# Weight-pair sums in nine steps with their rests on VectorE, and the input's sums made beside the second mLSTM head

## The chip, the cores and the metric

The kernel runs on one core of a Trainium2 chip. A core has five engines with an instruction queue each: TensorE (PE; its weight loads are shown as PEld), VectorE (DVE), ScalarE (ACT), GpSimd (POOL) and SyncE (SP), which here issues most of the DMAs. The metric is the device time of one execution in microseconds, as a median over runs.

## What is computed

One inference step of a hybrid decoder layer: an RMS norm, one input projection `w_in`, then two groups of heads side by side (four mLSTM heads, four HGRN2 heads), an output projection and a SwiGLU feed-forward layer. It is done for a prompt (1 x 1024 tokens) and for samples (8 x 4 tokens) that carry a state.

```python
h = _rmsnorm(x, norm_mix)
p = jnp.einsum('btd,dp->btp', h, w_in) + b_in
qk_a, v_a, o_a, i_a, f_a, q_b, f_b, i_b, g_b = jnp.split(p, offs, axis=-1)
out_a, buf, C, n, m = _mlstm_mixer(qk_a, v_a, o_a, i_a, f_a, conv_buf, C0, n0, m0, conv_w, conv_b, mlstm_norm)
out_b, S = _hgrn_mixer(q_b, f_b, i_b, g_b, S0, lb, hgrn_norm)
mix = jnp.concatenate([out_a, out_b], axis=-1).astype(x.dtype)
x = x + jnp.einsum('btm,md->btd', mix, w_out)
h2 = _rmsnorm(x, norm_ffn)
ff = jax.nn.silu(jnp.einsum('btd,df->btf', h2, w_gate)) * jnp.einsum('btd,df->btf', h2, w_up)
x = x + jnp.einsum('btf,fd->btd', ff, w_down)
```

The change lies in the input projection `w_in` and in what prepares its operands.

## The kernel before

All matrix products are done in fp32 precision by three passes of a rounded format: each operand is cut into a rounded part (`HI`, `whi`) and its rest (`LO`, `wlo` = operand minus rounded part), and PE does HI x whi (L168), LO x whi (L169), HI x wlo (L170). ACT makes the rounded part, and DVE or POOL subtracts to make the rest.

The weights come as tiles of 128 x 1024. `load` issues the DMA of a tile to one of two `raw` buffers (L105, on SP); `split` rounds it in two halves (L96 on ACT) and takes the rests (L97, on POOL or DVE). A tile's load can only go out when all readers of an earlier tile in its raw buffer are through. `nexts` says which tile is loaded after which.

PE's work is a list of units, one per weight tile and token block (1056 tokens in blocks of 288, 384 and 384). `emit_k` issues a unit's matmuls, and after every second step of k calls `hook`, which advances the side work: Python generators (heads, splits, sums) that issue instructions to the other engines and then say with `yield n` after how many hooks they want to go on. So the place of a `yield` sets where in each engine's queue an instruction stands. All engines work their queues in order.

The units go through the four mLSTM heads first (up to about 305 us), then the HGRN heads (up to about 600 us), then the output projection and the feed-forward layer. For the HGRN heads a pair of weight tiles and two token blocks are multiplied by a Strassen scheme of seven products. It needs sums of the inputs and sums of the weights:

- `x1_prep` makes the input's sums T1, T2 and T4 in four turns: it stores part of the input to DRAM (`d_b`), loads blocks of it into tiles that the heads use too (`qB`, `kB`; L1082), adds them (L1085, L1091 on DVE), rounds (L1089 on ACT) and takes the rest (L1092, on POOL). `x3_prep` makes T3 in the same way (L1107 to L1111). `x1_prep` is started 18 units before the first HGRN unit, which is beside the third and fourth mLSTM head.
- `pairs_split` makes the weights' sums S1 to S4 in place in the two raw buffers (L137, L141, L142, L146 on DVE), rounds them (L134 on ACT) and takes their rests (L135 on POOL), in four steps. At its end it loads the next two tiles (called x0 and x1 below). There are six such pairs, starting at about 305, 349, 385, 420, 455 and 490 us.

Of the products, P2's results go to two outputs (`put` L1139 or L1141 on ACT, then `add` L1145 on DVE), P5's are put by ACT (L1139 or L1141), and P3 then goes on in the PSUM bank of P5. Between these products stand the steps of the HGRN heads: decays and products on DVE (L854, L856, L862, L864), small matmuls on PE (L835, L913, L918, L937, L953, L975).

`sample_core` finishes a head for the samples (transpose at L740). `sample_a` does the mLSTM samples: small loads on SP (L754 to L757), then DVE steps (L763, L767, L768) that PE needs (L617). L586 is a memset of one column of `vt` on POOL, L604 a copy of the state C on DVE, L763 the first sample step.

Of the kernel before, what the change touches and what calls it, by code (L numbers as in the profile page):

```python
# [9 lines left out]
F32 = mybir.dt.float32  # L10
# [3 lines left out]
OP = mybir.AluOpType  # L14
# [26 lines left out]
def hybrid_step(ctx: ExitStack, tc: tile.TileContext, i, o):  # L41
    nc = tc.nc
# [9 lines left out]
    def bank(tag="mx"):  # L52
        return psum.tile([128, 512], F32, tag=tag, name=tag, bufs={"mm": 3, "mx": 4, "so": 1}[tag])

    units, tiles, nexts = [], [], {}
# [4 lines left out]
    def start(gen, key, wait=1):  # L60
        active.append([gen, key, wait])
# [12 lines left out]
    def finish(key):  # L74
        while key not in done:
            hook()

    NW, NRAW = 5, 2
    raws, his, los = {}, {}, {}

    def load(t):
        tag = {2: "wlo", 3: "whi"}.get(t, "raw")
        raws[t] = wp.tile([128, 1024], F32, tag=tag, name=tag, bufs=NRAW if tag == "raw" else NW)
        tiles[t](raws[t])
# [18 lines left out]
    def wtile(src, n=1024):  # L103
        def f(raw):
            nc.sync.dma_start(raw[:, :n], src)  # L105
        tiles.append(f)
        tile_n[len(tiles) - 1] = n
        return len(tiles) - 1
# [14 lines left out]
    def pairs_split(tb, ta, raw_a, raw_b):  # L123

        while ("w", raw_b) not in done:
            yield 1
        ra, rb = raws[raw_a], raws[raw_b]
        a11, a12, a21, a22 = ra[:, 0:512], ra[:, 512:1024], rb[:, 0:512], rb[:, 512:1024]

        def rnd(t, s, src):  # L130
            if t not in his:
                his[t] = wp.tile([128, 1024], F32R, tag="whi", name="whi", bufs=NW)
                los[t] = wp.tile([128, 1024], F32R, tag="wlo", name="wlo", bufs=NW)
            nc.scalar.activation(his[t][:, s], src, AF.Copy)  # L134
            nc.gpsimd.tensor_tensor(los[t][:, s], src, his[t][:, s].bitcast(F32), op=OP.subtract)  # L135
        left, right = slice(0, 512), slice(512, 1024)
        nc.vector.tensor_tensor(a22, a21, a22, op=OP.add)  # L137
        yield 1
        rnd(tb, right, a22)
        done.add(("S1", tb))  # L140
        nc.vector.tensor_tensor(a21, a11, a21, op=OP.subtract)  # L141
        nc.vector.tensor_tensor(a11, a22, a11, op=OP.subtract)  # L142
        yield 1
        rnd(ta, left, a11)
        done.add(("S2", tb))
        nc.vector.tensor_tensor(a12, a12, a11, op=OP.subtract)  # L146
        yield 1
        rnd(ta, right, a12)
        done.add(("S4", tb))
        yield 1  # L150
        rnd(tb, left, a21)
        done.add(("S3", tb))
        for x in nexts.get(ta, ()):
            load(x)

    def emit_k(u, ks):
        t, nk = u["t"], u["nk"]
# [123 lines left out]
    def tl(tag, n=384, bufs=2, dt=F32, p=128):  # L281
        n, bufs = 385 if tag == "kB" else n, 3 if tag == "go" else bufs
        return mp.tile([p, n], dt, tag=tag, name=tag, bufs=bufs)
# [253 lines left out]
    def norm_cols(s, sqs, nch, d2=None, p=128):  # L537

        if d2 is None:
            nc.vector.tensor_scalar(s[:p, :nch], sqs[:p, :nch], 1.0 / 128, EPS, op0=OP.mult, op1=OP.add)  # L540
        else:
            nc.vector.tensor_scalar_mul(d2[:p, :nch], d2[:p, :nch], EPS)
            nc.vector.scalar_tensor_tensor(s[:p, :nch], sqs[:p, :nch], 1.0 / 128, d2[:p, :nch],
                                           op0=OP.mult, op1=OP.add)
        nc.gpsimd.tensor_tensor(s[:p, :nch], s[:p, :nch], mhalf[:p, :nch], op=OP.pow)
# [100 lines left out]
    def sample_core(h_off, w, vnorm, st_in, decay, out_state, n_io, d2, k_scale, later=None):  # L646
# [86 lines left out]
            nc.scalar.activation(sm[:, 1, 0:1], pO[:, 128:129], AF.Square)  # L733
            nc.vector.tensor_tensor(sm[:, 1, 0:1], sm[:, 1, 0:1], d2, op=OP.max)
        norm_cols(sm[:, 2], sm[:, 0], 1, sm[:, 1] if d2 is not None else None)
        yield 2
        nc.vector.tensor_scalar_mul(hn, pO[:, 0:128], sm[:, 2, 0:1])
        yield 1
        pH = bank()
        nc.tensor.transpose(pH[:, 0:128], hn, ident)  # L740
        yield 1
# [254 lines left out]
    def sample_b():  # L996
        yield from sample_core(4, 128, V_HN, i["S0"], lambda h, s: gS[:, h, s:s + 1], o["Ss"], None, None, None,
                               later=("su",))
# [15 lines left out]
    for h in range(H):  # L1014
        ts = [wtile(wa[1 + 4 * h + j]) for j in range(4)]
# [15 lines left out]
    first_b = len(units)  # L1031
# [20 lines left out]
    def xop(name):  # L1052
        def blk(b, h_):
            o_ = KT * OFF[b] + 1536 * h_
            return lambda kk: (HI[:, o_ + 384 * kk:o_ + 384 * kk + 384], LO[:, o_ + 384 * kk:o_ + 384 * kk + 384])

        def tx(j):
            return lambda kk: tuple(TX[0][:, 1536 * (2 * j + x) + 384 * kk:1536 * (2 * j + x) + 384 * kk + 384] for x in (0, 1))

        def t4(kk):  # L1060
            return TX[0][:, 6144 + 384 * kk:6528 + 384 * kk], \
                TX[0][:, 7680 + 384 * kk:8064 + 384 * kk] if kk < 2 else t4x[0][:, 384 * kk - 768:384 * kk - 384]
        return {"B11": blk(1, 0), "B21": blk(1, 1), "T3": blk(2, 0), "B22": blk(2, 1), "T1": tx(0), "T2": tx(1), "T4": t4}[name]
# [9 lines left out]
    def x1_prep():  # L1073

        nc.sync.dma_start(d_b[0], HI[:, 5376:6912].bitcast(F32))
        nc.sync.dma_start(d_b[1], LO[:, 5376:6912].bitcast(F32))
        TX.append(act.tile([128, KT * T], F32R, tag="X", name="TX"))
        t4x.append(mp.tile([128, 768], F32R, name="t4x"))
        for kk in range(4):
            ts = [tl(x)[:, :384] for x in ("qB", "kB", "qB", "kB")]  # L1080
            for t, (m, c) in zip(ts, ((kk, 0), (kk, 384), (kk + 4, 0), (kk + 4, 384))):
                nc.sync.dma_start(t, d_n[:, m, c:c + 384])  # L1082
            b11, b12, b21, b22 = ts
            yield 6
            nc.vector.tensor_tensor(b12, b12, b11, op=OP.subtract)  # L1085
            for n_, t, a in (("T1", b12, b22), ("T2", b22, b21), ("T4", b21, None)):
                yield 1
                h, lw = xop(n_)(kk)
                nc.scalar.activation(h, t, AF.Copy)  # L1089
                if a is not None:  # L1090
                    nc.vector.tensor_tensor(a, a, t, op=OP.subtract)  # L1091
                nc.gpsimd.tensor_tensor(lw, t, h.bitcast(F32), op=OP.subtract)  # L1092
                yield 1
            yield 1

    def x3_prep():

        for kk in range(0, 4, 2):
            ts = [tl(x)[:, :384] for x in ("qB", "kB", "qB", "kB")]
            for j in range(2):  # L1100
                nc.sync.dma_start(ts[2 * j], d_n[:, kk + j, 384:768])
                nc.sync.dma_start(ts[2 * j + 1], d_n[:, kk + j + 4, 384:768])
            yield 7
            while ("pb",) not in done:
                yield 1
            for j in range(2):
                nc.vector.tensor_tensor(ts[2 * j], ts[2 * j + 1], ts[2 * j], op=OP.subtract)  # L1107
                yield 1
                h, lw = xop("T3")(kk + j)
                nc.scalar.activation(h, ts[2 * j], AF.Copy)  # L1110
                nc.gpsimd.tensor_tensor(lw, ts[2 * j], h.bitcast(F32), op=OP.subtract)  # L1111

    def x_back():

# [791 lines left out]
    for v in virt.values():  # L1906
        if v:
            tb, ta, ra, rb = v
# [78 lines left out]
    def next_splits(ui):  # L1987
        nonlocal nxt
        while nxt < n_t1 and t_split[nxt] <= ui:
            if nxt in virt:  # L1990
                if virt[nxt]:
                    start(pairs_split(*virt[nxt]), ("w", nxt))
            else:
                start(split(nxt, True), ("w", nxt), {3: 3, 4: 10}.get(nxt, 1))
            nxt += 1
            if nxt - 1 in virt:
                continue
            if t_split[nxt - 1] >= first[nxt - 1] - 1:
                finish(("w", nxt - 1))

    for ui, u in enumerate(units + [None]):
# [97 lines left out]
            finish(u["need"])  # L2099
        elif u["t"] > 1:  # L2100
            finish(("w", u["t"]))
        if ui == first_b - 18:
            start(x1_prep(), ("x1",))
        if ui == first_b - 1:
            finish(("x1",))
            start(x3_prep(), ("x3",))
# [28 lines left out]
        if first_ff <= ui < units1:  # L2135
# [14 lines left out]
            if k in (GSK, GSK + 2):  # L2150
                j = (k - GSK) // 2
# [88 lines left out]
```

## Time and profile before

| what | value |
|---|---|
| runs | 1431.28, 1434.98, 1435.43 us; median 1434.98 |
| profiled execution | 1431.96 us, its span 1430.1 us |
| mean granted clock of PE | 0.967 |
| PE busy | 1339.4 us, 94% of the span |
| DVE busy | 936.2 us, 65% |
| ACT busy | 585.9 us, 41% |
| POOL busy | 646.8 us, 45% |

The span is that of the profiled execution, and what lies around it is 1.9 us. The rows of the profile are of these kinds. A timeline row has the start in microseconds, the duration, the engine, the line, the operation with output and inputs, and in brackets, where the engine stood idle before, for how long and for whose result (`<-DVE kt L944`). "x4" says that four like instructions are drawn together, and `SPq` is the queue of SP, that is, the issue of DMAs. A group row has a line, its shapes, its count, and after the bar the busy time in microseconds and the mean of one in nanoseconds. Matmuls are pipelined, so their durations overlap: a matmul of 384 columns starts 0.17 us after the one before it at full clock.

### The profile page before, as it was taken

To read this page: it belongs to the slowest core of one execution; us is meant where nothing else is said; L and a number is where in the kernel's file an instruction comes from. 1 tells how busy PE (TensorE), PEld (TensorE's weight loads), DVE (VectorE), ACT (ScalarE), POOL (GpSimd) and SP (SyncE) were. 2 spreads that over 40 slices of the span, in tenths; PEclk is the share of its full clock that TensorE was granted. 3 is DMA by queue.
4 is the path that set the end of the run, shared out by engine and by line. 5 is a ranking of instruction groups with operands and counts; after the bars stand their busy time and mean duration, and the time that the engine had idled before them with its cause. 6 is when DMAs were issued, how large, how long until landed. Compare 5 with 4: busy or idle time off the path is not lost.

```text
span 1430.1 us, 29548 instructions
## 1 busy us (share of the span) xinstructions
PE 1339.4 (94%) x11528; PEld 1303.9 (91%) x11528; DVE 936.2 (65%) x2118; ACT 585.9 (41%) x1367; POOL 646.8 (45%) x606
## 2 busy tenths in 40 slices
PE   7879998798888999899998999999999999999996
PEld 6879998797888889799998999999999999999995
DVE  7876667667767766753556666666566336777775
ACT  6554334234444453512434555454444341222232
POOL 5323215344334431402536665666656584544434
PEclk7999999899999999999999999999999999999997
DMA  6212233241111161544463656666666268877843
GB/s 220 97 60 87 72 127 104 83 139 34 35 41 47 44 219 47 181 135 138 137 207 123 229 216 229 230 244 220 223 221 203 64 216 323 299 285 278 297 150 122
DMA packets 118724, 229.71 MB, mean 161 GB/s; under 512 B 11680, under 2 KB 72120, under 8 KB 118072
## 3 DMA queue, kind: packets, MB, share of 16 engines
q1 hardware_dynamic: 118152, 227.55, 46.0%
q8 instruction: 91, 1.49, 0.4%
q14 instruction: 49, 0.40, 0.1%
q10 hardware_dynamic: 432, 0.27, 0.1%
HBM read 153.33 MB, written 74.45 MB: 159 GB/s over the span
## 4 chain that ended last, share of the span: by engine, by line
PE 69%; DVE 16%; ACT 5%; issue 4%; DMA 3%; POOL 2%; SPq 0%; POOLq 0%; DVEq 0%; ACTq 0%
PE mx L1513 15%; PE mm L1513 9%; PE mm L168 8%; PE mm L169 7%; PE mm L170 7%; PE mx L1736 7%; PE mm L1736 4%; PE so L1513 3%; DMA rg<-d_ff 1%; PE mx L690 1%; PE mx L835 1%; ACT HI L272 1%; DVE X L271 1%; PE so L1736 1%; PE mm L1777 1%
## 5 line engine op out<-in xcount | busy, mean ns | idle before, releaser
L168 PE MATMUL mm<-HI,whi 128*128 128x384 f32 (+2 forms) x1064 | 348.5, 328 | 5.7 <-ACT qB L349 2.9
L170 PE MATMUL mm<-HI,wlo 128*128 128x384 f32 (+2 forms) x1064 | 334.4, 314 | 1.3 <-POOL wlo L97 1.3
L169 PE MATMUL mm<-LO,whi 128*128 128x384 f32 (+2 forms) x1064 | 334.4, 314 | 0.6 <-DVE LO L1246 0.3
L168 PEld LDWEIGHTS mm<-HI,whi 128*128 128x128 f32 x1064 | 206.1, 194 | 10.7 <-ACT qB L349 3.2
L170 PEld LDWEIGHTS mm<-HI,wlo 128*128 128x128 f32 x1064 | 206.2, 194 | 1.8 <-POOL wlo L97 1.8
L169 PEld LDWEIGHTS mm<-LO,whi 128*128 128x128 f32 x1064 | 206.4, 194 | 1.4 <-DVE LO L1246 0.6
L97 POOL TENSOR_TENSOR wlo<-raw,whi 128x512 fp32r<-128x512 f32 x90 | 118.9, 1332 | 179.0 <-ACT whi L96 146.5
L1442 POOL TENSOR_TENSOR wlo<-S,whi 128x512 fp32r<-128x512 f32 x78 | 109.6, 1411 | 92.8 <-ACT whi L1441 89.7
L1513 PE MATMUL mx<-T,whi 128*128 128x264 f32 x640 | 118.2, 284 | 0.0
L1566 POOL TENSOR_TENSOR LO<-rg,HI 128x528 fp32r<-128x528 f32 x52 | 71.1, 1379 | 65.9 <-ACT HI L1565 65.9
L1513 PEld LDWEIGHTS mx<-T,whi 128*128 128x128 f32 x640 | 99.0, 188 | 0.0
L1513 PE MATMUL mx<-HI,whi 128*128 128x264 f32 x320 | 91.1, 285 | 0.2 <-ACT u L1521 0.2
L1513 PE MATMUL mx<-HI,wlo 128*128 128x264 f32 x320 | 90.9, 284 | 0.0
L1513 PE MATMUL mx<-T,wlo 128*128 128x264 f32 x320 | 90.9, 284 | 0.0
L1513 PE MATMUL mx<-LO,whi 128*128 128x264 f32 x320 | 90.7, 283 | 0.0
L1654 DVE TENSOR_TENSOR fh<-fr,fh 128x512 fp32r<-128x512 f32 x80 | 67.9, 849 | 32.3 <-ACT fh L1649 31.8
L1740 DVE TENSOR_TENSOR X<-X,mx 128x264 f32<-128x264 f32 x160 | 65.4, 424 | 26.2 <-PE mx L1736 25.5
L1441 ACT ACTIVATE whi<-S 128x512 fp32r<-128x512 f32 x80 | 50.3, 630 | 69.4 <-DVE S L1430 65.6
L1565 ACT ACTIVATE HI<-rg 128x528 fp32r<-128x528 f32 x52 | 32.3, 642 | 105.2 <-PE mx L1736 32.1
L1513 PE MATMUL mm<-HI,wlo 128*128 128x264 f32 x240 | 68.2, 284 | 0.0
L1513 PE MATMUL mm<-HI,whi 128*128 128x264 f32 x240 | 68.2, 284 | 0.0
L1513 PE MATMUL mm<-LO,whi 128*128 128x264 f32 x240 | 67.9, 283 | 0.0
(584 smaller groups left out, 3698.3 us busy)
## 6 DMA issues: line engine op xcount, KB each, us to landing
d_wf<-fh SPq DMA_DIRECT2D x60, 512.0 KB
rg<-d_ff SPq DMA_DIRECT2D x42, 528.0 KB
raw<-in_wA SPq DMA_DIRECT2D x31, 512.0 KB
whi<-d_wf SPq DMA_DIRECT2D x29, 512.0 KB
wlo<-d_wf SPq DMA_DIRECT2D x28, 512.0 KB
raw<-in_wgu SPq DMA_DIRECT2D x24, 512.0 KB
d_ff<-sg SPq DMA_DIRECT2D x40, 264.0 KB
rg<-in_wgu SPq DMA_DIRECT2D x20, 512.0 KB
```

The source lines that it names most:

```text
L97: (nc.gpsimd if pool else nc.vector).tensor_tensor(lo[:, s], raw[:, s], hi[:, s].bitcast(F32), op=OP.subtract)
L168: nc.tensor.matmul(ps[:, :n], wh, rh[:, k, :], start=(k == 0 and not u["acc"]), stop=False, skip_group_check=sk)
L169: nc.tensor.matmul(ps[:, :n], wh, rl[:, k, :], start=False, stop=False, skip_group_check=sk)
L170: nc.tensor.matmul(ps[:, :n], wl, rh[:, k, :], start=False, stop=(k == nk - 1), skip_group_check=sk)
L1441: nc.scalar.activation(hi[:, s], t, AF.Copy)
L1442: (nc.vector if dve else nc.gpsimd).tensor_tensor(lo[:, s], t, hi[:, s].bitcast(F32), op=OP.subtract)
L1513: nc.tensor.matmul(ps[:, :QN], a[:, w], b_[:, kk, c], start=new and kk == 0 and x == 0, stop=kk == 3 and x == 2, skip_group_check=True)
L1565: nc.scalar.activation(h, src, AF.Copy)
L1566: (nc.vector if dve else nc.gpsimd).tensor_tensor(lw, src, h.bitcast(F32), op=OP.subtract)
L1654: nc.vector.tensor_tensor(lw, src, h.bitcast(F32), op=OP.subtract)
L1736: nc.tensor.matmul(ps[:, :QN], a[:, w], b_[k][:, cs], start=new and k == 0 and x == 0, stop=k == 1 and x == 2, skip_group_check=True)
L1740: nc.vector.tensor_tensor(y, y, ps[:, :QN], op=OP.add)
```

## The change

Four things are changed. (1) `pairs_split` goes on in nine steps instead of four: each rounding on ACT and each rest has its own step, the rests are taken on DVE (L137 in the numbers of the changed file), and the first of the two next loads is issued after the rest of S4, the second after the rest of S3. (2) `x1_prep` starts 35 units ahead of the first HGRN unit instead of 18, which is beside the second mLSTM head, with rests on DVE and twice the hooks between its steps. (3) `x3_prep` takes its rests on DVE, a hook later. (4) `sample_core` lets 3 and 4 hooks pass instead of 2 and 1, so that its transpose stands later on PE.

```diff
 def pairs_split(tb, ta, raw_a, raw_b):
...
             nc.scalar.activation(his[t][:, s], src, AF.Copy)
-            nc.gpsimd.tensor_tensor(los[t][:, s], src, his[t][:, s].bitcast(F32), op=OP.subtract)
+
+        def rest(t, s, src):
+            nc.vector.tensor_tensor(los[t][:, s], src, his[t][:, s].bitcast(F32), op=OP.subtract)
         left, right = slice(0, 512), slice(512, 1024)
         nc.vector.tensor_tensor(a22, a21, a22, op=OP.add)
         yield 1
         rnd(tb, right, a22)
+        nc.vector.tensor_tensor(a21, a11, a21, op=OP.subtract)
+        yield 1
+        rest(tb, right, a22)
         done.add(("S1", tb))
-        nc.vector.tensor_tensor(a21, a11, a21, op=OP.subtract)
+        yield 1
         nc.vector.tensor_tensor(a11, a22, a11, op=OP.subtract)
-        yield 1
         rnd(ta, left, a11)
+        yield 1
+        rest(ta, left, a11)
         done.add(("S2", tb))
+        yield 1
         nc.vector.tensor_tensor(a12, a12, a11, op=OP.subtract)
-        yield 1
         rnd(ta, right, a12)
+        yield 1
+        rest(ta, right, a12)
         done.add(("S4", tb))
+        x0, x1 = nexts[ta]
+        load(x0)
         yield 1
         rnd(tb, left, a21)
+        yield 1
+        rest(tb, left, a21)
         done.add(("S3", tb))
-        for x in nexts.get(ta, ()):
-            load(x)
+        load(x1)
...
 sample_core:
         norm_cols(sm[:, 2], sm[:, 0], 1, sm[:, 1] if d2 is not None else None)
-        yield 2
+        yield 3
         nc.vector.tensor_scalar_mul(hn, pO[:, 0:128], sm[:, 2, 0:1])
-        yield 1
+        yield 4
...
 x1_prep:
             for n_, t, a in (("T1", b12, b22), ("T2", b22, b21), ("T4", b21, None)):
-                yield 1
+                yield 2
...
-                nc.gpsimd.tensor_tensor(lw, t, h.bitcast(F32), op=OP.subtract)
-                yield 1
-            yield 1
+                yield 2
+                nc.vector.tensor_tensor(lw, t, h.bitcast(F32), op=OP.subtract)
+            yield 2
...
 x3_prep:
                 nc.vector.tensor_tensor(ts[2 * j], ts[2 * j + 1], ts[2 * j], op=OP.subtract)
-                yield 1
                 h, lw = xop("T3")(kk + j)
                 nc.scalar.activation(h, ts[2 * j], AF.Copy)
-                nc.gpsimd.tensor_tensor(lw, ts[2 * j], h.bitcast(F32), op=OP.subtract)
+                yield 1
+                nc.vector.tensor_tensor(lw, ts[2 * j], h.bitcast(F32), op=OP.subtract)
...
-        if ui == first_b - 18:
+        if ui == first_b - 35:
             start(x1_prep(), ("x1",))
```

Lines below `pairs_split` have numbers higher by 11 in the changed file (L1141 is L1152, L754 is L765, L856 is L867).

How the queues are changed by it, at three places. The first is SP's queue late in the third mLSTM head, before: loads of `x1_prep` (L1082) stand between the head's loads (L534, L535) and those of `sample_a` (from L754).

```order
L611 DMA out_Cp<-C 128x128
L534 DMA ngb<-d_bc 128x256
L535 DMA wib<-d_bc 128x256
L1082 DMA qB<-d_n 128x384
L1082 DMA kB<-d_n 128x384
L1082 DMA qB<-d_n 128x384
L1082 DMA kB<-d_n 128x384
L754 DMA ngS<-d_bc 32x32
L756 DMA wiS<-d_bc 128x32
L754 DMA ngS<-d_bc 32x32
```

After, the same place:

```order
L622 DMA out_Cp<-C 128x128
L545 DMA ngb<-d_bc 128x256
L546 DMA wib<-d_bc 128x256
L765 DMA ngS<-d_bc 32x32
L767 DMA wiS<-d_bc 128x32
L765 DMA ngS<-d_bc 32x32
L767 DMA wiS<-d_bc 128x32
L765 DMA ngS<-d_bc 32x32
```

The loads of `x1_prep` (L1093 now) are gone from here, and `sample_a` follows directly behind the head's loads.

The second is ACT's queue in the second pair (the one at 349 us), before. L134 rounds a sum, L96 rounds a half of a newly loaded tile, L1141 puts a product's results: the first is P2's, the second P5's.

```order
L134 ACTIVATE whi<-raw 128x512
L96 ACTIVATE whi<-raw 128x512 x2
L1141 ACTIVATE v<-mm,vec 128x384
L859 ACTIVATE qw<-qB 128x24x8
L860 ACTIVATE ck<-kB 128x24x8
L96 ACTIVATE whi<-raw 128x512
L1141 ACTIVATE go<-mm,vec 128x384
L981 ACTIVATE kt,sm<-mx 128x128 x2
```

And after:

```order
L134 ACTIVATE whi<-raw 128x512
L96 ACTIVATE whi<-raw 128x512
L1152 ACTIVATE v<-mm,vec 128x384
L134 ACTIVATE whi<-raw 128x512
L870 ACTIVATE qw<-qB 128x24x8
L871 ACTIVATE ck<-kB 128x24x8
L96 ACTIVATE whi<-raw 128x512 x2
L1152 ACTIVATE go<-mm,vec 128x384
```

P2's put stands now between the rounding of x0's first half and that of S3; the second half of x0 and the first of x1 stand together ahead of P5's put.

The third is DVE's queue in the same pair, before, from the addition of P2's results on (L1145):

```order
L1145 TENSOR_TENSOR v<-v,mm 128x384
L961 COPY C<-mx 128x128
L963 SCALAR_TENSOR_TENSOR C<-C,wib,mx 128x128
L842 COPY_PREDICATED AD_126<-msk,mx 128x24x2
L842 COPY_PREDICATED AD_126<-msk,mx 128x12x4
L854 TENSOR_TENSOR qB<-qB,wib 128x48x4
L856 TENSOR_TENSOR kB<-kB,wib 128x48x4
L862 TENSOR_TENSOR wib<-wib 128x48
L854 TENSOR_TENSOR qw<-qB,wib 128x24x8
L856 TENSOR_TENSOR ck<-kB,wib 128x24x8
L862 TENSOR_TENSOR wib<-wib 128x24
```

And after, down to the rest of S3 (L137):

```order
L1156 TENSOR_TENSOR v<-v,mm 128x384
L972 COPY C<-mx 128x128
L974 SCALAR_TENSOR_TENSOR C<-C,wib,mx 128x128
L853 COPY_PREDICATED AD_126<-msk,mx 128x24x2
L853 COPY_PREDICATED AD_126<-msk,mx 128x12x4
L865 TENSOR_TENSOR qB<-qB,wib 128x48x4
L867 TENSOR_TENSOR kB<-kB,wib 128x48x4
L873 TENSOR_TENSOR wib<-wib 128x48
L865 TENSOR_TENSOR qw<-qB,wib 128x24x8
L867 TENSOR_TENSOR ck<-kB,wib 128x24x8
L873 TENSOR_TENSOR wib<-wib 128x24
L137 TENSOR_TENSOR wlo<-raw,whi 128x512
```

The rest of S3 stands behind the addition (L1156 now) and ten further steps of the HGRN head; those of S1, S2 and S4 stand ahead of these rows. No rest of a weight sum was in this queue before.

More of the change, by code (lines that the diff above doesn't have):

```diff
@@ L139, in pairs_split @@
         rnd(tb, right, a22)
+        nc.vector.tensor_tensor(a21, a11, a21, op=OP.subtract)
+        yield 1
+        rest(tb, right, a22)
         done.add(("S1", tb))
-        nc.vector.tensor_tensor(a21, a11, a21, op=OP.subtract)
+        yield 1
         nc.vector.tensor_tensor(a11, a22, a11, op=OP.subtract)
+        rnd(ta, left, a11)
         yield 1
-        rnd(ta, left, a11)
+        rest(ta, left, a11)
         done.add(("S2", tb))
+        yield 1
         nc.vector.tensor_tensor(a12, a12, a11, op=OP.subtract)
+        rnd(ta, right, a12)
         yield 1
-        rnd(ta, right, a12)
+        rest(ta, right, a12)
         done.add(("S4", tb))
+        x0, x1 = nexts[ta]
+        load(x0)
         yield 1
         rnd(tb, left, a21)
+        yield 1
+        rest(tb, left, a21)
         done.add(("S3", tb))
-        for x in nexts.get(ta, ()):
-            load(x)
+        load(x1)
     def emit_k(u, ks):
```

## Prediction

> **What bounds the kernel now.** I read the page first: its span and the busy shares.
>
> ```profile
> span 1430.1 us, 29548 instructions
> ...
> PE 1339.4 (94%) x11528; PEld 1303.9 (91%) x11528; DVE 936.2 (65%) x2118; ACT 585.9 (41%) x1367; POOL 646.8 (45%) x606
> ```
>
> PE sets the time; what can be won is the 6% in which it idles, and matmuls run at a low clock. The windows say where that is, for the stages the change touches (columns: stretch, its length, PE, PEld, DVE, ACT, POOL busy, granted clock, DMA share, GB/s).
>
> ```profile
> 125.00:225.00 100.00, 100.00 (x664) 99.86 (x663) 65.24 (x173) 39.87 (x109) 26.73 (x35) 1.00 0.29 94
> 230.00:235.00 5.00, 3.58 (x21) 3.58 (x22) 2.27 (x7) 0.60 (x2) 3.56 (x5) 0.79 0.24 58
> 255.00:260.00 5.00, 1.30 (x8) 0.79 (x6) 2.40 (x15) 0.87 (x4) 0.00 (x0) 1.00 0.67 203
> 260.00:265.00 5.00, 1.19 (x10) 0.70 (x10) 4.69 (x12) 1.80 (x5) 3.44 (x9) 0.52 0.08 30
> 265.00:270.00 5.00, 5.00 (x22) 4.87 (x19) 4.25 (x13) 1.62 (x7) 0.71 (x2) 0.50 0.01 2
> 345.00:370.00 25.00, 22.31 (x273) 20.94 (x272) 18.42 (x43) 13.32 (x37) 12.64 (x12) 0.93 0.13 44
> 360.00:365.00 5.00, 5.00 (x25) 5.00 (x25) 2.86 (x11) 3.00 (x7) 2.62 (x3) 0.74 0.36 108
> 395.00:400.00 5.00, 5.00 (x25) 4.60 (x20) 1.73 (x3) 2.85 (x7) 3.13 (x3) 0.50 0.49 156
> ```
>
> From 125 to 225 us, where the first two mLSTM heads run, PE has no gap at all. In 255 to 265 it works 2.5 us of 10 and then runs at half clock until 270. Around the weight pairs (360, 395) it is busy again but slow, since it stood just before. PE's waits name what it stood for (start, duration, instruction, and in brackets the idle time and its releaser):
>
> ```profile
> 231.42 0.94 PE L596 MATMUL mx<-vt,kt 128*128 128x129 f32 x6 [2.52 <-POOL vt L586]
> 249.19 0.27 PE L760 MATMUL mx<-sq,sk 128*32 128x32 f32 x8 [1.29 <-DVE kt L588]
> 258.75 0.71 PE L617 MATMUL mx<-vt,W 128*128 128x129 f32 x4 [3.16 <-DVE PB L767]
> 263.81 0.80 PE L619 MATMUL mx<-C,qw 128*128 128x129 f32 x2 [4.36 <-DVE C L604]
> 357.71 0.68 PE L953 MATMUL mx<-vt,kt 128*128 128x128 f32 x4 [2.53 <-DVE kt L944]
> 391.45 0.38 PE L913 MATMUL mx<-qw,ck 128*32 128x32 f32 x12 [1.73 <-DVE ck L856]
> 394.63 0.85 PE L918 MATMUL mx<-qB,kB 128*32 128x64 f32 x12 [2.80 <-DVE wib L862]
> ```
>
> The first four lie in the stage of the third and fourth mLSTM head, where the input's sums (x1_prep) are made now; the others each lie in a weight pair.
>
> **Part 1, the input's sums move to the second head.** What they did at the old place shows on three engines:
>
> ```profile
> 230.21 1.11 POOL L1092 TENSOR_TENSOR TX<-kB,TX 128x384 fp32r<-128x384 f32 x1
> ...
> 225.97 6.97 SPq L105 DMA_DIRECT2D raw<-in_wA  x2
> ...
> 236.44 0.48 SPq L535 DMA_DIRECT2D wib<-d_bc  x1
> ...
> 250.82 0.42 SPq L1082 DMA_DIRECT2D kB<-d_n  x1
> ...
> 255.04 0.43 SPq L757 DMA_DIRECT2D nT<-in_n0T  x1
> ...
> 256.85 0.25 DVE L763 SCALAR_TENSOR_TENSOR sW<-ngS,scol,cst 128x32 f32<-128x32 f32 x1 [5.70 <-DMA nT<-in_n0T]
> ```
>
> SP is a queue in order. The loads of the fourth turn of x1_prep (L1082) wait there until the tiles of an earlier turn come free; the last issues at 250.82, so the loads of sample_a behind it, from L754 on, end with L757 at 255.04. DVE stands 5.70 us for that one (L763), then PE 3.16 us for L767 and 4.36 us for L604, which is further down on DVE. After the change the L754 row follows right behind L535, issued at 236.44, so DVE goes on at about 251.2, where it began its idle time (256.85 less 5.70). PE can have L619 some 5.8 us earlier, at about 258 instead of 263.81. With only one stall of some 2 to 3 us left, half or all of the half-clock stretch goes too: it holds about 6 us of matmul at 0.50, which is 3 us lost. Sum here -8.8.
> At 231.42 PE waited 2.52 us for a memset (L586): it stood in POOL's queue behind the rests of x1_prep (L1092) and one of the weights. Without x1_prep's rests that wait goes, and with it the slow stretch at 0.79 (1.5 us or less): -4. The 1.29 us at 249.19 stand for L588, behind L1091 on DVE: -1.2. Together -14; ends -10 (the slow stretches stay) and -16 (all gone).
>
> What it costs at the new place: twelve sums, as before, and twelve rests that now also come on DVE.
>
> ```profile
> L268 DVE TENSOR_TENSOR LO<-X,HI 128x384 fp32r<-128x384 f32 x6 | 3.5, 576 | 0.6 <-ACT HI L272 0.2
> L1246 DVE TENSOR_TENSOR LO<-X,HI 128x528 fp32r<-128x528 f32 x8 | 5.5, 701 | 1.4 <-ACT HI L1245 1.3
> ```
>
> No rest of this shape is on DVE now; the same operation, form and width is L268, 576 ns. Twelve are 6.9 us, with the sums 13.7 us, spread over about 80 us in which DVE is free for a third (65.24 of 100 busy). PE has full cover there, so at best nothing is lost. What could be: the two stores of x1_prep and sixteen loads are in SP's queue among the loads for the heads, and a sum that waits for its load holds up the head's own steps behind it on DVE. PE's one wait of this kind today is 1.29 us (249.19); I take 1.5, ends 0 and 4. If the cover of PE's queue were gone, the whole 13.7 would count, which nothing in that stretch suggests. The rests of x3_prep (four, by 576) and the later two transposes in sample_core stand in the same stretch as the first pair; I put nothing on them beyond what that pair gets below.
>
> **Part 2, the pairs in nine steps.** The rests leave POOL for DVE. What that frees, seen on the first pair of the second kind:
>
> ```profile
> 349.22 1.50 DVE L137 TENSOR_TENSOR raw<-raw 128x512 f32<-128x512 f32 x1
> 350.75 0.69 DVE L141 TENSOR_TENSOR raw<-raw 128x512 f32<-128x512 f32 x1
> ...
> 356.76 2.84 SPq L105 DMA_DIRECT2D raw<-in_wA  x2
> ...
> 357.96 1.27 POOL L135 TENSOR_TENSOR wlo<-raw,whi 128x512 fp32r<-128x512 f32 x1 [0.66 <-ACT whi L134]
> ...
> 360.05 1.15 ACT L96 ACTIVATE whi<-raw 128x512 fp32r<-128x512 f32 x2 [2.17 <-DMA raw<-in_wA]
> 361.11 0.56 ACT L1141 ACTIVATE v<-mm,vec 128x384 f32<-128x384 f32 x1
> 361.70 0.56 DVE L1145 TENSOR_TENSOR v<-v,mm 128x384 f32<-128x384 f32 x1 [2.35 <-ACT v L1141]
> 364.49 0.17 DVE L862 TENSOR_TENSOR wib<-wib 128x24 f32<-128x24 f32 x1
> ...
> 364.16 0.62 ACT L96 ACTIVATE whi<-raw 128x512 fp32r<-128x512 f32 x1
> 364.68 0.56 ACT L1141 ACTIVATE go<-mm,vec 128x384 f32<-128x384 f32 x1
> ...
> 367.18 0.33 PE L168 MATMUL mm<-HI,whi 128*128 128x384 f32 x1
> ```
>
> A sum takes 0.69 us alone (L141) and 1.50 when POOL is at work (L137): the two shut each other out. With rests at 0.70 on DVE (L1246 is slightly wider) in place of 1.3 on POOL, DVE's work per pair grows by 2.8 us less the excess of its own steps, some 2 to 4 us. The HGRN steps between (L854, L856, L862) then come as early as now or earlier, so the waits at 357.71, 391.45 and 394.63 shrink by 1 to 2.7 us.
>
> But two loads of weights hang on the rests. A load needs its raw buffer, and that comes free when the pair's last reader of it is through. Now the first load (x0) goes out at 356.76, as POOL ends the rest of S4, 7.5 us after the pair's first sum, and the second (x1) about when the rest of S3 ends, 357.96 + 1.27 = 359.2, or 10.0 after it. ACT takes x0 up at 360.05, 3.3 us after its issue, having waited 2.17 us for it.
> In the new order S4's rest is DVE's, behind S2's rest, S4's sum and its rounding. Replayed with these durations it ends 9.6 to 9.9 us after the first sum, so x0 can be rounded at 13.0 (9.75 + 3.3) instead of 10.8. P2's results (L1141 at 361.11) stand behind that on ACT, so they come at 13.6 to 14.1; then the rounding of S3. And S3's rest on DVE stands behind the addition of those results (L1145) and ten steps of the head, which take from 361.70 to 364.66 now: 14.1 + 2.96 + 0.7 = about 17.7. Only then is x1 loaded, and it can be rounded at 21.0 (17.7 + 3.3). P5's result (L1141, go, at 364.68) stands on ACT behind the first half of x1 (L96 at 364.16), now as before; it is then out at 22.2 instead of 16.0. P3 adds into the same PSUM bank, so it must wait for it: 22.3 instead of 367.18 - 349.22 = 17.96. That is +4.3. What shrank earlier in the pair doesn't help, since this is a time counted from the pair's first sum and set by the two loads.
> The last pair of this kind has 17.63 (below), the middle one 16.36 likewise, so their losses are +4.7 and +5.9: +15 for three.
>
> ```profile
> 490.25 1.50 DVE L137 TENSOR_TENSOR raw<-raw 128x512 f32<-128x512 f32 x1
> ...
> 507.88 0.33 PE L168 MATMUL mm<-HI,whi 128*128 128x384 f32 x1
> ...
> 396.17 1.15 ACT L96 ACTIVATE whi<-raw 128x512 fp32r<-128x512 f32 x2 [3.55 <-DMA raw<-in_wA]
> ...
> 405.14 0.33 PE L168 MATMUL mm<-HI,whi 128*128 128x384 f32 x1
> ```
>
> The other kind (two pairs, the first at 385) has more matmuls between: x0 is already late now (ACT waits 3.55 us at 396.17) and comes about 1.5 us later, x1 at about 406, and P3 moves from 405.14 to about 407: +2 each, +4. In the first pair of all, at 305, P3's kin come about level with now: +1. Sum over six pairs +20. Ends: +8, if the loads land in 2.5 us and the replay's DVE is 1 us quicker at each link, and +28, if each of the new stalls brings a slow stretch of its own like the 0.74 in 360 to 365 (5 us x 0.26 = 1.3 us, some six times).
>
> On that last end the Trainium skill has a rule (TensorE: Matmul & The Clock Gate, Part 1): the clock halves after an idle window of about 3.4 us. By it new stalls of up to 3.3 us would cost no clock, and the upper end would be +20. The row at 357.71 speaks against it here: after 2.53 us of idle time the clock of 360 to 365 was 0.74.
>
> **Sum:** -14 + 1.5 + 20 = +7.5 us on the profiled execution, which took 1431.96 us around its span of 1430.1: 1439.5. The median of the three runs, 1434.98, lies 3.0 above it, so I expect 1442 there.
>
> **Rivals.** *The loads aren't what P3 waits for (faster).* If rests come in time on DVE, so that x1 is rounded before P5 ends, the pairs gain what contention costs them: of the waits at 357.71 (2.53), 391.45 and 394.63 (4.53) about 1 to 2.5 per pair of the second kind and 2.7 of the first, and one slow stretch each of 1.3 to 2.5: some -10 to -14. With part 1 at -12.5 the time is 1435 - 25 = about 1411. It needs S3's rest to end before about 12.5 us after the first sum (16.0 less 3.3 and 0.6 of rounding, plus slack of P3), that is, DVE must not hold it behind L1145. For it: POOL's rests of 1.27 do become 0.70. Against: the order, where the rest stands after L1145. By the Trainium skill (SBUF — State Buffer, Who interferes with whom) an instruction of VectorE with two inputs in SBUF and one of GpSimd that reads SBUF block each other fully; the 1.50 beside 0.69 above agrees, and that rule is what would carry this case.
> *Gain and loss cancel (same).* The loads cost only the second kind, +10 to +12, and the heads give -12: within 4.3 us (0.3%, about what a measurement of this kernel can tell from no change). Time 1434.
> *DVE becomes the bound.* DVE has 18.42 us of 25 busy around a pair (345 to 370). If POOL's rests were added to it without the contention going away, each pair loses a further 2 and x1_prep beside the second head costs 4: 1442 + 14 = about 1455. Against: the 65.24 of 100.
> *The move doesn't unblock sample_a,* because SP's queue is held by other loads at that place (two of weights held it from 225.97 for 6.97 us): then the -8.8 falls away and the time is 1451.
>
> **How the numbers follow.** Forecast 0.45, gain without the load's wait 0.25, cancelling 0.2, DVE or SP in the way 0.1. The forecast of 1442 has its own range 1432 to 1452, so about a quarter of it lies within 0.3% of 1434.98 and the rest above. Faster 0.31 (0.25, and a third of the cancelling case), same 0.24, slower 0.45. The range leaves out the best of the first rival and half of the last two: 1415 to 1454.
>
> **What would show it.** In the trace after: in the pairs of the second kind the two raw loads of a pair issue about 8 us apart (2.5 now), ACT waits for a raw load ahead of both results, and P3 starts 20 to 23 us after the pair's first sum. No sum in a pair takes over 0.8 us. PE's waits for L586, L767 and L604 near 231 and 258 to 264 are gone or below 2 us, and 260 to 270 runs at over 0.8. From 125 to 225 PE keeps 98 or more of 100. If P3 starts 18 us or less after the first sum, the forecast is wrong, and the first rival right; if DVE still waits for nT near 256, part 1 is wrong.

## The result and the profile after

The changed kernel takes 1450.63 us (median of four runs, 1448.79 to 1452.79); the kernel before, on the same chip, 1434.65 (four runs, 1431.28 to 1435.43). The ratio is 1.0117 with a 95% interval of 1.0095 to 1.0138: 16 us slower, where the prediction had 7. The profiled execution took 1452.79 us, the longest of the four, so the two traces lie 20.8 us apart where the medians lie 16.0 apart; 3 us of that are ahead of 97 us, in the start, whose instructions are unchanged.

The page of the changed kernel, span and busy shares:

```profile
span 1451.0 us, 29523 instructions
...
PE 1347.2 (93%) x11528; PEld 1308.4 (90%) x11528; DVE 940.0 (65%) x2158; ACT 584.9 (40%) x1367; POOL 600.8 (41%) x566
```

PE does the same 11528 matmuls, but is busy 7.8 us longer, though nothing was added to it. The windows where the input's sums were made before:

```profile
125.00:225.00 100.00, 99.01 (x655) 98.12 (x654) 75.09 (x195) 42.59 (x118) 23.64 (x31) 1.00 0.33 107
230.00:235.00 5.00, 5.00 (x40) 5.00 (x39) 3.94 (x8) 2.14 (x5) 2.57 (x3) 1.00 0.40 123
255.00:260.00 5.00, 4.31 (x33) 3.99 (x34) 4.11 (x12) 1.10 (x6) 0.54 (x4) 1.00 0.00 0
260.00:265.00 5.00, 5.00 (x38) 4.55 (x37) 3.58 (x12) 1.67 (x3) 1.71 (x5) 1.00 0.19 56
265.00:270.00 5.00, 5.00 (x39) 4.55 (x39) 4.46 (x17) 1.10 (x2) 1.67 (x7) 1.00 0.34 105
```

That stage is as good as forecast: no stall, full clock. In the trace of the changed kernel the small load that DVE stood for goes out early, and one short wait of PE is left:

```profile
240.76 0.43 SPq L768 DMA_DIRECT2D nT<-in_n0T  x1
...
255.69 0.49 PE L630 MATMUL mx<-C,qw 128*128 128x129 f32 x2 [1.55 <-DVE C L615]
```

The results of the same unit come 2.95 us later than before at 156 us, 4.10 later at 192, and 11.12 us earlier at 303 (times of the kernel before). So the new place cost 1.15 and the old one gave 15.2 back: -14.1 in all.

All of the loss lies in the weight pairs. The same stretch of work, from the same unit's results to the same unit's, in the kernel before and then in the changed one:

```profile
303.60:535.90 232.30, 207.59 (x2509) 194.28 (x2509) 164.73 (x451) 106.39 (x299) 95.86 (x89) 0.94 0.24 77
```

```profile
292.50:555.80 263.30, 217.00 (x2510) 199.91 (x2510) 163.11 (x479) 106.13 (x299) 60.38 (x61) 0.91 0.21 69
```

It takes 31.0 us more. PE's idle time grows from 24.7 to 46.3 us, +21.6; and the same matmuls, 2509 and 2510 of them, take 9.4 us more, at a granted clock of 0.91 for 0.94. DVE works no longer than before (163.11 for 164.73), though it has 24 rests more. PE's long waits in the first pair of all, in the first pair of the second kind and the first of the other kind, and in the last pair:

```profile
320.10 0.69 PE L179 MATMUL mm<-TX,whi 128*128 128x384 f32 x1 [4.74 <-DVE cq L532]
...
355.51 0.49 PE L986 MATMUL mx<-C,qB 128*128 128x128 f32 x2 [2.85 <-DVE C L972]
...
362.88 0.44 PE L179 MATMUL mm<-HI,whi 128*128 128x384 f32 x1 [2.60 <-ACT go L1152]
...
397.97 0.87 PE L948 MATMUL mx<-ident,kB 128*128 128x128 f32 x3 [6.01 <-DVE kB L867]
...
524.54 0.69 PE L179 MATMUL mm<-HI,whi 128*128 128x384 f32 x1 [3.96 <-ACT go L1152]
```

In the first pair the kernel before had a long wait too, 3.73 us at 325.69 for `sample_core`'s transpose (L740).

What they wait for leads to ACT. These are its rows around the second pair (first sum at 341.35), with the two loads on SP:

```profile
350.30 8.34 SPq L105 DMA_DIRECT2D raw<-in_wA  x2
```

```profile
353.57 0.63 ACT L96 ACTIVATE whi<-raw 128x512 fp32r<-128x512 f32 x1 [4.02 <-DMA raw<-in_wA]
354.10 0.56 ACT L1152 ACTIVATE v<-mm,vec 128x384 f32<-128x384 f32 x1
...
361.73 0.63 ACT L96 ACTIVATE whi<-raw 128x512 fp32r<-128x512 f32 x1 [3.97 <-DMA raw<-in_wA]
362.27 0.56 ACT L1152 ACTIVATE go<-mm,vec 128x384 f32<-128x384 f32 x1
```

The loads go out 8 us apart. ACT stands 4 us for each, and right behind it in its queue is a result that PE needs: P2's at 354.10, P5's at 362.27. In the groups of instructions from 300 to 545 us ACT waits 49.2 us for raw loads ahead of L96, where it was 17.0 before:

```profile
L96 ACT ACTIVATE whi<-raw 128x512 fp32r<-128x512 f32 x25 | 15.6, 625 | 49.2 <-DMA raw<-in_wA 49.2
```

### The profile page after: what moved, and what is told of

The parts are those of the page before. It is cut to its first block, busy times and chain, and to the rows that moved or that the text cites. A ratio compares the mean times of both kernels' runs of the same rounds, so it can differ in the third digit from the quotient of the medians.

```text
span 1451.0 us, 29523 instructions
## 1 busy us (share of the span) xinstructions
PE 1347.2 (93%) x11528; PEld 1308.4 (90%) x11528; DVE 940.0 (65%) x2158; ACT 584.9 (40%) x1367; POOL 600.8 (41%) x566
## 3 DMA queue, kind: packets, MB, share of 16 engines
q8 instruction: 91, 1.49, 0.5%
## 4 chain that ended last, share of the span: by engine, by line
PE 69%; DVE 15%; ACT 5%; DMA 5%; issue 4%; POOL 2%; SPq 0%; POOLq 0%; DVEq 0%; ACTq 0%
PE mx L1524 15%; PE mm L1524 9%; PE mm L179 8%; PE mm L181 8%; PE mm L180 8%; PE mx L1747 7%; PE mm L1747 4%; PE so L1524 3%; DMA raw<-in_wA 2%; DMA rg<-d_ff 2%; PE mx L701 1%; PE mx L846 1%; PE so L1747 1%; ACT whi L96 1%; DVE wlo L137 1%
## 5 line engine op out<-in xcount | busy, mean ns | idle before, releaser
L96 ACT ACTIVATE whi<-raw 128x512 fp32r<-128x512 f32 x90 | 54.2, 622 | 50.1 <-DMA raw<-in_wA 50.1
```

What stands on the lines that cost most here:

```text
L96: nc.scalar.activation(hi[:, s], raw[:, s], AF.Copy)
```

## The experiments

All ratios below are to the kernel before, run in the same turns. Its median was 1433.17 to 1435.38 us in the several groups of turns, so times of different groups compare to some 2 us only. Line numbers in the rows of a version are its own.

**The parts alone.** First the pairs without the rest of the change (`pairs_split` of the changed kernel in the kernel before), then `x1_prep` without the rest.

> Only the weight pairs are changed (nine steps, rests on VectorE, the later loads); the input's sums, x3_prep and sample_core stay as before. My theory: the pairs alone lose 31 us, as the drift between the two traces shows from 303 us on (-11.1 to +19.9), of which about 21 us is idle time of PE and 8 to 10 us is matmuls at a low clock after the new stalls; so 1435 + 31 = 1466 us, and the granted clock is below 0.93 in the pairs' windows. Rival: the loss comes from both parts together (the pairs lose only because the earlier heads bring them 11 us earlier, before their loads): then the pairs alone lose about the 20 us of the prediction, 1455 us.

> Only x1_prep is changed (started at the second mLSTM head, its rests on VectorE, two hooks between its steps). My theory: the heads gain what the two traces show between 156 and 303 us, +1.2 at the new place and -15.2 at the old one: 1435 - 14 = 1421 us, with PE's waits for L586, L767 and L604 gone. Rival: the gain at the old place needs x3_prep's rests off GpSimd or the later transposes too: then less than 10 us, 1426 us or more.

Measured: 1463.18 us (1.0189, 1.0163 to 1.0214) and 1421.71 us (0.9905, 0.9881 to 0.9930). Against 1435.38 that is +27.8 and -13.7. They add up to +14.1, and the whole change was +16.0 (1450.63 less 1434.65), so `x3_prep`, `sample_core` and what the parts do to each other come to 2 us in sum. Both rivals fall.

**Order or engine.** The same steps with the rests on GpSimd again, and a kernel with S3 early:

```diff
 e4_nine_pool: in rest()
-            nc.vector.tensor_tensor(los[t][:, s], src, ...)
+            nc.gpsimd.tensor_tensor(los[t][:, s], src, ...)
```

```diff
 e3_s3_early: in pairs_split, with the rests on VectorE
         rest(tb, right, a22)
         done.add(("S1", tb))
+        rnd(tb, left, a21)
+        yield 1
+        rest(tb, left, a21)
+        done.add(("S3", tb))
...
         done.add(("S4", tb))
-        x0, x1 = nexts[ta]
-        load(x0)
-        yield 1
-        rnd(tb, left, a21)
-        yield 1
-        rest(tb, left, a21)
-        done.add(("S3", tb))
-        load(x1)
+        for x in nexts[ta]:
+            load(x)
```

> The changed kernel with the same nine steps and the same places of the loads, but the rests of the weight sums are taken on GpSimd again. My theory: the steps' order costs, not the engine: S3's rest still stands behind P2's results, so the second load still goes out 7 to 8 us after the first, PE still waits about 2 to 4 us for the put of P5, and the sums and steps on VectorE are slowed by GpSimd (over 1 us where now 0.69): 1450 to 1458 us. Rival (the engine costs): 1435 us or less, as the rests no longer stand in VectorE's queue.

> The changed kernel, but S3 is rounded and its rest taken on VectorE right after the rest of S1 (ahead of the sum S2), in eight steps, and both next loads are issued after the rest of S4. The rests are all still on VectorE. My theory: what costs is that the second load hangs on S3's rest behind P2's results. Then both loads issue within 1 us, PE's waits for the put of P5 (2.60, 2.68 and 3.96 us) go, P3 starts at most 18.5 us after the first sum of the pair in the pairs of the second kind, and the time falls by about 20 us (15 of lateness, some 5 of low clock) to about 1430 us. Rival: the rests on VectorE cost by themselves, since they hold up the head's steps: then P3 comes as late as now and the time stays within 5 us of 1450.

Measured: 1442.59 us with the rests on GpSimd (1.0054, 1.0038 to 1.0070), 1415.32 with S3 early (0.9865, 0.9839 to 0.9891). For the first both numbers missed: the order holds some 21 of the pairs' 28 us (1442.59 less the 1421.71 of `x1_prep` alone), the place of the rests on VectorE the other 7. With GpSimd PE still waits for P5's put, but 0.83, 0.81 and 0.27 us only, since S3's rest no longer stands behind the head's steps; the wait for P2's results is 3.1 us (5.3 in the other kind). With S3 early both kinds of wait are gone from the five later pairs, but for one of 1.85 us (the first pair keeps its 4.74 us), and the time is 15 us better than expected. The loads are 3.6 us apart and not 1: the first one goes out at 346.46, 6.3 us after the first sum, just when S2's sum (to 346.40) has read the other buffer, that of S1 and S3, for the last time. By these times x0 takes that buffer, and it comes earlier after the first sum than in the kernel before (6.3 us for 7.5) and the changed one (9.0):

```profile
346.46 3.94 SPq L105 DMA_DIRECT2D raw<-in_wA  x2
...
349.61 0.63 ACT L96 ACTIVATE whi<-raw 128x512 fp32r<-128x512 f32 x1 [0.30 <-DMA raw<-in_wA]
350.14 0.56 ACT L1149 ACTIVATE v<-mm,vec 128x384 f32<-128x384 f32 x1
```

So there are three orders of the steps and two engines. What was still open are the four steps of before with the rests on VectorE, and S3 early with the rests on GpSimd:

```diff
 e6_four_dve: pairs_split of the kernel before in the changed kernel
-            nc.gpsimd.tensor_tensor(los[t][:, s], src, ...)
+            nc.vector.tensor_tensor(los[t][:, s], src, ...)
```

```diff
 e7_s3_pool: in rest() of the kernel with S3 early
-            nc.vector.tensor_tensor(los[t][:, s], src, ...)
+            nc.gpsimd.tensor_tensor(los[t][:, s], src, ...)
```

> The changed kernel with the four steps of before in the weight pairs (sums ahead, each rest right behind its rounding, both loads at the end), but the rests on VectorE. My theory: the order costs, not the engine: both loads go out within 4 us of each other, PE has no wait over 1 us for the put of P5, and the time is 1412 to 1424 us, as with the input's sums moved alone (1421.7) or a little better for the contention that goes. Rival: rests on VectorE behind the roundings hold up the head's steps: 1430 us or more.

> The kernel of the run with S3 early (1415.3 us), but with the rests of the weight sums on GpSimd. My theory: taking them to VectorE is worth something once the loads don't hang on it: with GpSimd at work the sums take 1.1 us and more again and the head's steps come later, so 1420 to 1428 us. Rival: the engine is without effect here: 1413 to 1418 us.

Measured: 1424.59 us (0.9941, 0.9921 to 0.9960) and 1419.13 (0.9891, 0.9871 to 0.9911). Each against the kernel before in its turns, in us:

| order of the steps | rests on VectorE | rests on GpSimd |
|---|---|---|
| four, as before | -10.0 | -13.7 (`x1_prep` alone) |
| nine | +16.0 (the change) | +7.2 |
| S3 early | -20.1 | -15.5 |

The order of the steps moves the time by some 35 us on one engine. The engine is worth 9 us against VectorE in nine steps and 5 us for it with S3 early. In four steps the two cells differ in more than the engine, since the run with `x1_prep` alone has `x3_prep` and `sample_core` as before: its PE waits 3.84 us at `sample_core`'s transpose (L740 at 312.55), and the run beside it has no such wait. So what the engine alone is worth there isn't shown. Both runs just missed their ranges (1412 to 1424, and 1420 to 1428), and neither my theories nor the rivals have the whole of it.

**The clock by itself.** Matmuls that nobody reads fill PE's waits in the changed kernel:

```diff
 e5_warm
+    def warm(n):
+        pw = bank("so")
+        x = xop("B11")(0)[0]
+        for _ in range(n):
+            nc.tensor.matmul(pw[:, :384], x[:, 0:128], x, start=True, stop=True)
...
 ahead of P3, in the pairs of the second kind:
+            warm(13)
...
 ahead of L948, in the pairs of the other kind:
+            warm(28)
...
 ahead of L986, in the pairs of the second kind:
+                    warm(14)
```

> The changed kernel with matmuls added whose results nobody reads (128x384, 0.17 us each), placed on PE where it stands waiting in the weight pairs: 14 ahead of L986 and 13 ahead of P3 in the three pairs of the second kind, 28 ahead of L948 in the two pairs of the other kind. 137 in all, 24 us of PE work that lies within waits of 2.6 to 6.0 us. My theory: about 8 of the pairs' 31 us are matmuls at half clock behind these waits; with PE at work the clock stays above 0.97 in the pairs' windows and the time falls by 4 to 8 us, to about 1444 us. Rival: the clock isn't what costs, since PE then waits for the heads' steps anyway: within 2 us of 1450.6, or slower by what the added matmuls overrun.

Measured: 1443.67 us (1.0068, 1.0055 to 1.0081), 7 us less than the changed kernel with 137 matmuls more. The windows from 300 to 560 us, of the changed kernel and of this one:

```profile
300.00:560.00 260.00, 213.70 (x2517) 196.95 (x2516) 159.92 (x470) 104.56 (x296) 58.38 (x55) 0.91 0.20 66
```

```profile
300.00:560.00 260.00, 229.24 (x2711) 212.91 (x2710) 164.69 (x484) 107.22 (x308) 62.04 (x58) 0.99 0.19 64
```

The clock is 0.99 for 0.91. So some 7 of the 9.4 us that PE was busy longer are shown to be the clock behind the waits. The first pair got no added matmuls; there the wait of 4.7 us is still followed by five microseconds at 0.50.

**ACT's queue by itself.** Loads, sums and rests stay as in the changed kernel; only the rounding of the loaded tiles is emitted later, first that of x1, then of both:

```diff
 e8_late_x1 (x1 only) and e9_late_both
         while t not in raws or (t and t - 1 not in his):
             yield 1
+        if t in late:
+            yield late[t]
...
 pairs_split:
+        late[nexts[ta][0]] = 3
+        late[nexts[ta][1]] = 5
```

> The changed kernel; only the rounding of x1 (the second of the two loaded tiles) is emitted 5 hooks later, so that on ACT it stands behind the puts of P5 and P6 instead of ahead of them. Loads, sums and rests are as in the changed kernel, x1 is loaded as late. My theory: P3 waits for P5's put only because that stands behind the rounding of x1 on ACT; then PE's waits of 2.60, 2.68 and 3.96 us at P3 and what they cost in clock go: about 9 + 4 = 13 us less than 1450.6, 1437 us. Rival: the late load itself costs, wherever its rounding stands, since the unit that uses x1 waits for it: within 4 us of 1450.6.

> As the run before, and the rounding of x0 is emitted 3 hooks later too, behind the put of P2. Loads, sums and rests as in the changed kernel. My theory: the waits ahead of P2's results (2.85 us at L986, 6.0 us at L948) go as well, and with them nearly all that the pairs lost: 1418 to 1426 us. Rival: these waits come from the rests on VectorE and not from ACT's queue: 1434 us or more.

Measured: 1441.75 us (1.0052, 1.0035 to 1.0068) and 1404.98 (0.9800, 0.9785 to 0.9815). Against 1450.63 that is 9 us and 46 us, the first less than expected, the second far more. With x1 late alone PE's waits for P5's put are gone, those for P2's results (2.8 to 6.0 us) stay, and each pair of the second kind has a new wait of 1.7 to 2.0 us: the late rests of x1 on GpSimd (1.4 us each), and a step that they push back there, now run beside two steps of the head on DVE, which take 1.15 and 1.41 us instead of 0.35 each. With both late there is none of the old waits, that of 4.74 us in the first pair included, and PE's longest wait in the pairs is 1.71 us. The chain behind that is closed in itself: x0's rounding held P2's results, S3's rounding and rest stand behind those, and x1's load waits for that rest. Take the first out, and the loads of the second pair are 4 us apart, at the same place in the program:

```profile
341.05 0.34 SPq L107 DMA_DIRECT2D raw<-in_wA  x1
...
345.13 0.34 SPq L107 DMA_DIRECT2D raw<-in_wA  x1
```

```profile
300.00:560.00 260.00, 240.69 (x3056) 223.56 (x3054) 195.10 (x570) 124.88 (x361) 72.31 (x80) 0.99 0.25 82
```

PE is busy 240.69 of 260 us there, against 234.30 before (more work falls into the window, as it is done earlier). This version beats the kernel before by 28 us (1433.17 in its turns) and the changed one by some 45.

**What is left.** S3 early and both roundings late; the kernel before with both roundings late and nothing else; both late with the rests on GpSimd. The edits are those above, in other pairings.

> The kernel with S3 early (1415.3 us), with the roundings of x0 and x1 emitted 3 and 4 hooks later, behind the puts of P2, P5. My theory: what is left of ACT's waits for loads (0.3 to 1.9 us in five pairs, 4.4 us in the first, where the wait of 4.74 us for L529 hangs on it) goes: 1406 to 1413 us. Rival: these waits lie beside others, and it stays within 3 us of 1415.

> The kernel before, with nothing of the change, but the roundings of x0 and x1 emitted 3 and 5 hooks later, behind the puts of P2 and P5. My theory: before, ACT waited 17.8 us in 7 places for these loads, but PE stood for head steps that GpSimd slowed, so most of that wait lies beside other work: 2 to 8 us faster, 1427 to 1433 us. Rival: ACT's queue was the pairs' bound before as well, and the gain is the 45 us that the same edit brings to the changed kernel, or a good part of it: below 1415 us.

> The kernel with both roundings late (1405.0 us), but the rests of the weight sums on GpSimd. My theory: with ACT's queue free, VectorE is the better place for the rests, since GpSimd slows the sums and the head's steps: 1410 to 1418 us. Rival: the engine has no effect: within 3 us of 1405.

Measured: 1413.83 us (0.9861, 0.9847 to 0.9876), 1433.00 (0.9986, 0.9975 to 0.9997) and 1408.01 (0.9819, 0.9800 to 0.9839).

With S3 early my range missed and the rival's number holds, but not as "these waits lie beside others". By the traces, one execution each, the first pair is 7.4 us shorter from its first sum to the next pair's (39.58 for 46.95), since the wait of 4.74 us goes, and the two pairs of the other kind are 2.5 and 1.4 us longer. Why this is then 9 us worse than the nine steps with the same edit can be read in part: PE idles 5.9 us more in the six pairs. In the pairs of the second kind it waits 1.3 to 1.7 us for `vt`, which stands on ACT behind the rounding of S2, and S2's sum comes later when S3 goes first (6.1 us after the pair's first sum for 5.3, in the pairs at 401 and 397 us). The rest is open.

In the kernel before the same edit brings 0.9 us, less than the 2 to 8 us of my theory and far from the rival's 45. The traces show a gain and a loss in it, again of one execution each, and that of the edit is the slowest of its ten runs (1435.84 us). The first pair is 5 us shorter (38.33 for 43.38), as PE's wait for L740 goes; the pairs at 349 and 490 us are 4.7 and 3.3 us longer, with a new wait of 2.02 us in each:

```profile
371.95 0.52 PE L943 MATMUL mx<-ident,kB 128*128 128x128 f32 x3 [2.02 <-DVE wib L868]
```

There, too, the late rests of x1 on GpSimd hold up two steps of the head on DVE (1.15 and 1.41 us for 0.35 each). In the other five pairs six of the seven waits over 1.2 us that the kernel before had stay (1.8 to 3.3 us), so ACT's queue wasn't what they hung on.

With both late and the rests on GpSimd the time is 1408.01 for 1404.98. That is less than the 5 to 13 us that I expected; the two intervals overlap, so an advantage of VectorE isn't shown here.

## Why the prediction was half right

The direction, the place and the mechanism were right; the sum was +7.5 us and is +16.

- The input's sums: -12.5 forecast (-14 and +1.5), -14.1 in the traces, -13.7 alone. SP's queue, the memset on GpSimd and the slow stretch went as described, and PE is busy 99.01 of 100 us at the new place.
- P3 behind the two loads: forecast 22.3 us after the pair's first sum in the three pairs of the second kind, measured 21.5 (362.88 - 341.35), 22.1 and 23.6 (524.54 less 500.99). P3 comes 15.2 us later in the three together, and the sum had 15.
- **The step that failed** is the clock in the term for the pairs. I put the slow stretches behind the new waits at zero and only into the upper end, +28 with six of 1.3 us each. In the traces the pairs cost 31.0 us and not 20: 21.6 of idle time, about as the sum had it, and 9.4 of matmuls at a lower clock, of which the added matmuls take 7 away. From first sum to first sum the three pairs of the second kind lose 5.3, 8.6 and 9.2 us, 23.1 together, so 7.8 more than P3's lateness; 8.8 of the 23.1 is PE being busy longer. The row I quoted (0.74 after a wait of 2.53 us) said so: each such pair now has two waits of that size or more where it had one. It belonged into the sum, which would have been +16.9 with the 9.4.
- The smaller terms: the two pairs of the other kind lose 2.5 and 2.2 us (+4 forecast). They lose no clock, since they ran at 0.90 before and run at 0.91 now. The first pair loses 3.3 us where I had +1; I had not seen that its results, too, stand behind x0's rounding on ACT (the wait of 4.74 us, which goes with both roundings late). That the sum with the 9.4 comes so near to the +16.0 of the medians is partly luck, as these terms and the input's sums are each off by 1 to 2 us and the traces lie further apart than the medians.
- "What shrank earlier in the pair doesn't help" held: the wait at 357.71 went from 2.53 to 0.32 us (347.62 in the trace after), and PE then stood 2.85 us longer further down.
- "No sum in a pair takes over 0.8 us" was wrong: the first sum of the second pair still takes 1.49 us, beside another step on GpSimd (L875, from 341.18 for 1.11 us). The sum of 1.50 us that I read as slowed by the rests had the same step beside it in the kernel before (L864, from 349.06 for 1.12 us), and no rest.
- The rival with the gain was real as a mechanism but not by its condition: what PE waited for was ACT's queue. With both roundings late S3's rest still stands behind the addition of P2's results and the load behind it goes out 13.0 us after the first sum (345.13 less 332.10), not before 12.5; even so the kernel comes to 1405, somewhat below the 1411 of that rival.

The Trainium skill (TensorE: Matmul & The Clock Gate, Part 1) has the clock halve after about 3.4 us of idle time. The trace here does not agree as far as one gap goes: PE waited 2.85 us until 355.51 and 2.60 until 362.88, and the five microseconds in which it went on had a clock of 0.66 each in the changed kernel:

```profile
355.00:360.00 5.00, 4.49 (x62) 3.97 (x62) 3.16 (x12) 1.34 (x4) 2.10 (x2) 0.66 0.17 34
...
362.00:367.00 5.00, 4.12 (x15) 4.12 (x16) 3.23 (x12) 4.91 (x16) 3.25 (x3) 0.66 0.00 0
```

By the rule, taken for a single wait, these would have cost no clock; by the measurement they do, and the measurement decides. The waits above 3.4 us agree with it: 0.50 in the five microseconds behind the 4.74 us at 320.10.

## What to carry to other kernels

When a step that frees a buffer is moved later, follow the load behind it to the engine that takes it up, and look at what stands behind that instruction in the engine's queue: here two roundings that waited 4 us each for their loads held a result each that PE needed, and moving these roundings three and five hooks later was worth some 45 us. Follow what you move as well: in the kernel before the same edit was worth 0.9 us, because it took a wait away in one pair and put late rests beside the heads' steps in others. And count a wait of PE twice, once for itself and once for the matmuls that may then run slow; here that began at waits of about 1.5 us.

## What the runs showed of the hardware

A wait of 2.85 us on PE was followed by some 3.4 us at half clock (0.50 from 356.50 to 359.90, where matmuls of 384 columns start 0.32 us apart and not 0.17), which is the 0.66 over five microseconds. Matmuls whose results are thrown away, put into such waits, kept the clock at 0.99 and made the kernel 7 us faster.

The length of one wait doesn't decide alone. In the kernel before the same instruction waited 2.32 us in two pairs, and only one of them was followed by a low clock:

```profile
428.76 0.68 PE L953 MATMUL mx<-vt,kt 128*128 128x128 f32 x4 [2.32 <-DVE kt L944]
...
498.53 0.68 PE L953 MATMUL mx<-vt,kt 128*128 128x128 f32 x4 [2.32 <-DVE kt L944]
```

```profile
428.76:433.76 5.00, 5.00 (x77) 4.85 (x77) 2.98 (x8) 1.79 (x4) 3.64 (x3) 1.00 0.68 235
498.53:503.53 5.00, 5.00 (x66) 4.84 (x67) 2.31 (x5) 1.91 (x4) 3.49 (x3) 0.66 0.74 227
```

In the fourteen traces, from 150 to 600 us, no wait of 1.2 to 1.48 us was followed by less than 1.00 in the next five microseconds. From 1.49 to 2.52 us both happened. After every wait of 2.53 us and more it was 0.72 or less, though some of these had another wait shortly before.

In the start, which is the same code, two profiled executions differ by 3 us.
